# Experts put in order of their tokens, with two products a block where they have at most 64

## The chip, the cores and the metric

The kernel runs on one core of one Trainium2 chip, as one program. The metric is the device time of one execution in microseconds (us), the median of several runs. A profile of one further execution gives the span from its first to its last instruction, and every instruction of each engine: TensorE (PE, its weight loads PEld), VectorE (DVE), ScalarE (ACT), GpSimd (POOL) and SyncE (SP), which issues the loads.

## What is computed

Two stacks of two layers each over 256 tokens of width 1024, in float32. The change concerns the last layer's mixture of experts: eight experts, each a gated feed forward with 3584 inner columns; every token takes the two experts with the largest router logits.

```python
def moe_ffn(h, router_w, router_b, w_gate, w_up, w_down):
    t = h.reshape(b * s, d)
    logits = (t @ router_w).astype(jnp.float32) + router_b.astype(jnp.float32)
    top_vals, top_idx = lax.top_k(logits, TOP_K)
    top_w = jax.nn.softmax(top_vals, axis=-1)
    gates = jnp.sum(jax.nn.one_hot(top_idx, N_EXPERTS) * top_w[..., None], axis=1)
    out = jnp.zeros((b * s, d), jnp.float32)
    for e in range(N_EXPERTS):
        y = swiglu_2(t, w_gate[e], w_up[e], w_down[e])   # (silu(t @ g) * (t @ u)) @ d
        out = out + gates[:, e:e + 1] * y
    return out
```

The inputs are drawn at random from a seed, the default being 0. 256 tokens with two experts each are 512 choices, 64 an expert on average.

## The kernel before

**Float32 from two halves.** The large products take operands rounded to a shorter format (F32R in the code) in place of plain float32. Each operand is split into a high part (its rounding) and a low part (what is left), and one product becomes three: high with high, low with high, high with low. For the weights this is `halves` (lines 323 to 333): from each load of 128 x 1024 floats (0.524 MB) ScalarE writes `hi` (line 331) and VectorE `lo` (line 332). Both pools have three buffers (`hip`, `lop`), and a buffer comes free when TensorE has read it.

**Loads.** `load_half` (line 314, the DMA on line 320) issues a load on SyncE's queue into the next buffer of a ring; the ring for the experts has 27 buffers, and 6 more for the first expert's first blocks (`rawd`, `rawf`). The weights' order in memory is that of their use, and their addresses are fixed in the program. A load waits until VectorE has read the buffer's last content.

**The stage.** `route` (line 1552) makes the residual with tokens on partitions (`ACC`), its normed rows as high and low parts (`HH`, `HL`), the router's logits, the gates `GT`, and `key`: the slot that each token has at each of its experts, from 1 on, else 0. `experts` (line 1667) goes through the experts in the order of their numbers. `gather` turns `key` into a one-hot matrix `OH` (tokens by slots, line 1691) and multiplies `HH` and `HL` by it, so that `XG` holds an expert's tokens in up to 128 slots, features on partitions, both parts. It runs for the first expert alone, then for the second, and then for two at a time. Then come seven blocks of 512 inner columns. `gate_up` makes the gate's and the other product of a block: 2 x 8 x 3 products of a 128 x 128 stationary `XG` tile with 512 moving columns of weights. `down` transposes the gated result (4 transposes), splits it into `hh` and `hl` and adds 2 x 4 x 3 products into the expert's output `ya`; it is issued one block late, behind the next block's `gate_up`. That is 72 products and 12 loads a block, whatever number of the 128 slots is filled. After the seventh block `scatter` splits `ya` (two splits), brings it back to token order with `OT`, the transposed one-hot (8 products), and adds it to `ACC` with the gate (four VectorE operations, line 1781).

`moe` (line 1809) reads the largest count into a register and runs a second pass, for slots 129 to 256, only where an expert has over 128 tokens. `final` is the last norm. The order of instructions on each engine is fixed when the program is built, by a planner; at run time each engine works through its queue in order, and semaphores do the rest.

Of the kernel before, what the change touches and what calls it, by code (L numbers as in the profile page):

```python
# [18 lines left out]
P = 128  # L19
S = 256  # L20
# [7 lines left out]
# ---------------------------------------------------------------- column layout of the packed vectors  # L28
# [29 lines left out]
NRB, NRC, NRD, NRE, NRF = 8, 12, 4, 3, 2  # L58

# ---------------------------------------------------------------- constants of the shapes  # L60
# [3 lines left out]
def _const_arrays():  # L64
# [30 lines left out]
    add("iota", np.broadcast_to(i[None, :] + 1, (P, P)))  # L95
    add("rev8", np.broadcast_to(8.0 - np.arange(8)[None, :], (P, 8)))
    add("dmask", np.where(i[:, None] <= i[None, :], 0.0, -1.0e30))
# [25 lines left out]
    # trailing means less the token itself: tokens s of a first tile to t of both, and of a second to its own  # L123
# [16 lines left out]
# ---------------------------------------------------------------- host layout  # L140
# [22 lines left out]
def _pack(inp):  # L163
# [9 lines left out]
    for l in range(2):  # L173
# [12 lines left out]
        # an even head's turned rows come after its others, an odd one's before  # L186
# [21 lines left out]
    # key and query, value, and gate tiles, in the order of the heads' work  # L208
# [34 lines left out]
# ---------------------------------------------------------------- kernel  # L243
class _K:
# [12 lines left out]
    # ---- tensor engine  # L257
# [21 lines left out]
    # ---- constants  # L279
# [27 lines left out]
    # ---- weights  # L307
# [15 lines left out]
    def halves(self, raw, parts=1):  # L323
        """A weight's two parts."""
# [28 lines left out]
    # ---- splits and norms  # L353
# [47 lines left out]
    def prep(self, gname, gi):  # L401
        """Splits of x * g for all feature tiles, and the row scale to apply after the product."""
# [9 lines left out]
    # ---- dense feed forward  # L412
# [35 lines left out]
    # ---- rope tables  # L448
    def rope_tables(self, pool):
        nc = self.nc  # L450
        with self.tc.tile_pool(name="rope", bufs=1) as rp:
# [17 lines left out]
            for j in range(4):  # L469
                # phase of a quarter turn for the cosines  # L470
# [71 lines left out]
    def weave(self, *gens):  # L542
        """Issues the steps of several generators in turn: next the one whose steps weigh least so far."""
# [35 lines left out]
    def track(self, tag, gen, weight=1.0, ahead=0):  # L579
        """Runs a generator's steps with their PSUM banks under one tag."""  # L580
# [15 lines left out]
    def seg(self, fn, *args, **n):  # L596
        """Runs a stage with PSUM banks besides the products' two: for each tag its number."""
# [1340 lines left out]
```

## Time and profile before

| What | us |
|---|---|
| Median of 3 runs | 2648.29 |
| Lowest and highest run | 2646.78, 2648.96 |
| Span of the profiled execution | 2645.7 |
| TensorE busy in that span | 2605.0 |
| VectorE busy | 2001.3 |
| ScalarE busy | 1610.3 |

The profiled execution has no time of its own besides its span; the span lies 2.6 us below the median of the runs, which also hold what lies before the first and after the last instruction. An engine's busy time counts its instructions' own spans; a TensorE record holds the latency of its product too, so that records overlap. `L332` is line 332 of the kernel before; a line may be a helper's, so groups are told apart by the names of tiles: `gu` and `y` are the two kinds of products of a block, `x` the small products (transposes, gather, scatter).

### The profile page before, as it was taken

Reading aid. Unit: us, or ns where it says so; the run is one execution under the profiler, and the core shown is the slowest. Engines: PE = TensorE matmul, PEld = TensorE weight load, DVE = VectorE, ACT = ScalarE, POOL = GpSimd, SP = SyncE. Lnnn points to the kernel's source line nnn. Section 1 sums busy time; section 2 is a strip of 40 time slices with the busy share of each in tenths; the row PEclk is TensorE's granted clock in tenths of the full one; section 3 lists DMA queues with packets and bytes.
Section 4 is the critical chain, followed back from the end, with each engine's and each line's share of the span. In section 5 each row is a group of like instructions: output and inputs, shape, how many; then the busy total and the mean of one; then the engine's idle time right before and its main releaser. Section 6 shows DMA issues by size and latency. Waiting matters only on the chain.

```text
span 2645.7 us, 44986 instructions
## 1 busy us (share of the span) xinstructions
PE 2605.0 (98%) x17519; PEld 2365.1 (89%) x17519; DVE 2001.3 (76%) x2624; ACT 1610.3 (61%) x2208; POOL 86.7 (3%) x85
## 2 busy tenths in 40 slices
PE   8999999999999999999999999999999999999997
PEld 8999899999999899999999988888888888888886
DVE  7658567656658577656666867898989898989897
ACT  5444455444444555455445766777777777777776
POOL 0003000000003000000000200000000000000000
PEclk9999999999999999999999999999999999999999
DMA  6554125555554125555555339899999999999992
GB/s 232 190 183 160 56 79 163 187 184 184 185 184 159 62 81 172 187 185 167 188 187 166 120 132 338 312 336 355 336 367 354 341 351 364 352 340 354 363 353 96
DMA packets 166621, 602.08 MB, mean 228 GB/s; under 512 B 18704, under 2 KB 19232, under 8 KB 166400
## 3 DMA queue, kind: packets, MB, share of 16 engines
q1 hardware_dynamic: 165792, 596.92, 64.5%
q8 instruction: 139, 2.28, 0.3%
q0 software_dynamic: 608, 2.21, 0.3%
q14 instruction: 82, 0.67, 0.1%
HBM read 596.96 MB, written 1.05 MB: 226 GB/s over the span
## 4 chain that ended last, share of the span: by engine, by line
PE 93%; issue 3%; DVE 2%; ACT 1%; DMA 0%; POOL 0%; DVEq 0%; SPq 0%; ACTq 0%; POOLq 0%
PE m L259 24%; PE mm L259 23%; PE gu L259 22%; PE y L259 11%; PE s L259 6%; PE t L259 3%; PE x L259 1%; PE x L277 1%; PE s L500 1%; DVE lo L332 1%; PE u L259 1%; ACT hi L331 0%; PE c L259 0%; PE s L277 0%; ACT xh L360 0%
## 5 line engine op out<-in xcount | busy, mean ns | idle before, releaser
L331 ACT ACTIVATE hi<-raw 128x1024 fp32r<-128x1024 f32 x1128 | 1176.1, 1055 | 824.2 <-issue 323.3
L332 DVE TENSOR_TENSOR lo<-raw,hi 128x1024 fp32r<-128x1024 f32 x1128 | 1356.0, 1222 | 422.7 <-ACT hi L331 417.7
L259 PE MATMUL gu<-hi,XG 128*128 128x512 f32 x1792 | 559.9, 397 | 0.1
L259 PE MATMUL m<-xh,hi 128*128 128x256 f32 x1760 | 495.2, 281 | 9.2 <-ACT xh L360 8.7
L259 PE MATMUL m<-xh,lo 128*128 128x256 f32 x1760 | 495.4, 282 | 3.0 <-DVE lo L332 3.0
L259 PE MATMUL m<-xl,hi 128*128 128x256 f32 x1760 | 494.9, 281 | 1.8 <-DVE xl L361 1.8
L259 PEld LDWEIGHTS gu<-hi,XG 128*128 128x128 f32 x1792 | 337.1, 189 | 80.3 <-ACT hi L331 0.6
L259 PE MATMUL gu<-lo,XG 128*128 128x512 f32 x896 | 348.0, 398 | 0.0
L259 PEld LDWEIGHTS m<-xh,hi 128*128 128x128 f32 x1760 | 333.0, 189 | 9.8 <-ACT xh L360 9.1
L259 PEld LDWEIGHTS m<-xh,lo 128*128 128x128 f32 x1760 | 332.9, 189 | 3.9 <-DVE lo L332 3.9
L259 PEld LDWEIGHTS m<-xl,hi 128*128 128x128 f32 x1760 | 332.7, 189 | 2.4 <-DVE xl L361 2.4
L259 PE MATMUL mm<-hl,hi 128*128 128x256 f32 x880 | 248.2, 282 | 0.0
L259 PE MATMUL mm<-hh,lo 128*128 128x256 f32 x880 | 248.2, 282 | 0.0
L259 PE MATMUL mm<-hh,hi 128*128 128x256 f32 x880 | 247.6, 282 | 0.0
L259 PE MATMUL mm<-xh,hi 128*128 128x256 f32 x832 | 240.8, 290 | 6.1 <-DVE x L1128 3.2
L259 PE MATMUL mm<-xl,hi 128*128 128x256 f32 x832 | 239.9, 289 | 0.0
L259 PE MATMUL mm<-xh,lo 128*128 128x256 f32 x832 | 238.2, 287 | 0.1
L259 PEld LDWEIGHTS gu<-lo,XG 128*128 128x128 f32 x896 | 169.0, 189 | 41.4 <-DVE lo L332 0.9
L259 PE MATMUL y<-lo,hh 128*128 128x512 f32 x448 | 181.0, 404 | 0.0
L259 PE MATMUL y<-hi,hh 128*128 128x512 f32 x448 | 177.7, 397 | 0.7 <-ACT hh L357 0.7
L259 PE MATMUL y<-hi,hl 128*128 128x512 f32 x448 | 178.0, 397 | 0.0
L259 PEld LDWEIGHTS mm<-hl,hi 128*128 128x128 f32 x880 | 168.2, 191 | 0.0
(551 smaller groups left out, 3448.3 us busy)
## 6 DMA issues: line engine op xcount, KB each, us to landing
raw<-in_moe SPq DMA_DIRECT2D x668, 512.0 KB, 5.3
raw<-in_ffn SPq DMA_DIRECT2D x330, 512.0 KB, 4.2
raw<-in_win SPq DMA_DIRECT2D x56, 512.0 KB, 3.6
raw<-in_dnin SPq DMA_DIRECT2D x32, 512.0 KB, 3.5
raw<-in_wout SPq DMA_DIRECT2D x16, 512.0 KB, 3.5
raw<-in_pin SPq DMA_DIRECT2D x8, 512.0 KB, 4.3
raw<-in_dnout SPq DMA_DIRECT2D x8, 512.0 KB, 3.6
raw<-in_moe SPq DMA_DIRECT2D x8, 256.0 KB, 5.5
```

What stands on the lines that cost most here:

```text
L259: ins = self.nc.tensor.matmul(out, lhsT=lhsT, rhs=rhs, start=start, stop=stop)
L277: self.nc.tensor.transpose(out, in_, self.c("ident"))
L331: nc.scalar.activation(hi[:, c], raw[:, c], AF.Copy)
L332: nc.vector.tensor_tensor(lo[:, c], raw[:, c], hi[:, c].bitcast(F32), OP.subtract)
L500: nc.tensor.transpose(p4[:, h, :].bitcast(F32R), YP[:, h, 1, :], self.identr)
```

## The change

`route` also counts: which experts have over 64 tokens, and in which order the experts stand by their count, the first kept first (it gets 2 x 256 added). Place p gets the expert of rank `PLACES[p]`, so ranks 1 and 2 stand at places 3 and 6; the six other places are those of `FEW`. The keys and gates are brought into the order of the places (`keyp`, `GTp`); `keyl` is the key with 64 added. Three kinds of numbers go into registers: the largest count, whether the new form is valid (`ok`: at most two experts over 64, the first not among them, and none over 128), and the experts of places 1 to 7, with which SyncE addresses the loads.

`short` is a new form of `experts`. At a place of few tokens the high parts of the tokens stand in slots 1 to 64 of the stationary tile and the low parts in slots 65 to 128, so that one product by the weights' high part makes two of the three, and one by the low part the third (and the fourth, low with low, which was left out before). The gate's two halves of rows are added by a plain float32 product with `BOTH` (twice the identity of 64) before the gating; `down` adds them in its transposes, which become plain float32 products of 64 columns, and packs high and low parts into `hh`; `scatter` adds the halves of the output, its one-hot having both. A block at such a place has 48 products and the added ones in place of 72. At the two other places nothing changes. Where `ok` is 0, the residual, which has been copied to memory, is loaded again, and the whole of `experts` runs as before in a further pass. The early ring has 31 buffers in place of 33 (`NRD` 3 for 4, `NRF` 1 for 2). `experts` is kept for the further pass, with one gather for each expert. Two constants are added (a tile of zeros and the places). All other lines of the diff take comments away.

```diff
-NRB, NRC, NRD, NRE, NRF = 8, 12, 4, 3, 2
+NRB, NRC, NRD, NRE, NRF = 8, 12, 3, 3, 1
+PLACES = (0, 3, 4, 1, 5, 6, 2, 7)
+FEW = [r not in (1, 2) for r in PLACES]
...
-        cm = self.T(keep, [P, 1], "cm")
-        nc.vector.tensor_reduce(cm, pc[:, 0:8], AX.X, OP.max)
-        ci = self.T(keep, [P, 1], "ci", I32)
-        nc.vector.tensor_copy(ci, cm)
+        cnt = self.T(pool, [P, NE], "cnt")
+        nc.vector.tensor_copy(cnt, pc[:, 0:8])
+        many = self.T(pool, [P, NE], "many")
+        nc.vector.tensor_scalar(many, cnt, 64.5, None, OP.is_gt)
+        cv = self.T(pool, [P, 4], "cv")
+        nc.vector.tensor_reduce(cv[:, 0:1], cnt, AX.X, OP.max)
+        nc.vector.tensor_reduce(cv[:, 2:3], many, AX.X, OP.add)
+        nc.vector.scalar_tensor_tensor(cv[:, 2:3], many[:, 0:1], 8.0, cv[:, 2:3], OP.mult, OP.add)
+        nc.vector.tensor_scalar(cv[:, 3:4], cv[:, 0:1], P + 0.5, None, OP.is_lt)
+        nc.vector.scalar_tensor_tensor(cv[:, 1:2], cv[:, 2:3], 2.5, cv[:, 3:4], OP.is_lt, OP.mult)
...
+        nc.vector.tensor_scalar(cnt[:, 0:1], cnt[:, 0:1], 2.0 * S, None, OP.add)
...
+        nc.vector.tensor_tensor(same, other, own, OP.is_equal)
+        nc.vector.tensor_tensor(more, other, own, OP.is_gt)
+        nc.vector.tensor_tensor(same, same, low, OP.mult)
+        nc.vector.tensor_tensor(more, more, same, OP.add)
...
+        nc.vector.tensor_reduce(crank, more, AX.X, OP.add)
...
+        nc.vector.tensor_tensor(at, crank[:, None, :].broadcast_to([P, NE, NE]),
+                                self.c("places")[:, :, None].broadcast_to([P, NE, NE]), OP.is_equal)
+        nc.vector.tensor_tensor(more, at, rev[:, None, :].broadcast_to([P, NE, NE]), OP.mult)
+        nc.vector.tensor_reduce(cnt, more, AX.X, OP.add)
+        nc.vector.tensor_scalar(ci[:, 2:], cnt, -1.0, 8.0, OP.mult, OP.add)
...
+        keyp = placed(key, "keyp")
...
+        nc.vector.tensor_scalar(keyl, keyp, 0.5, 64.0, OP.is_gt, OP.mult)
+        nc.vector.tensor_tensor(keyl, keyl, keyp, OP.add)
+        GTp = placed(GT, "GTp")
...
+    def short(self, HH, HL, ACC, RS, keyp, keyl, GTp, BOTH, where, st):
...
+                    nc.vector.tensor_scalar(OH[:, t, u, :], self.c("iota"), keyp[:, t, e:e + 1], None, OP.is_equal)
+                    nc.vector.tensor_scalar(OL[:, t, u, :], self.c("iota") if FEW[e] else self.c("zero"),
+                                            keyl[:, t, e:e + 1] if FEW[e] else 1.0, None, OP.is_equal)
...
+                    for i, (src, one) in enumerate(((HH, OH), (HL, OL))):
+                        for t in range(2):
+                            self.mm(ps, o, src[:, t, c], one[:, t].rearrange("p a b -> p (a b)"), i + t == 0, i + t == 2)
...
+        def gate_up(e, fb, XG, RX):
...
+                    ch = self.chunk(where(e)[fb * 6 + m * 2 + q])
...
+                        self.mm(ps, ps, XG[:, 0, k, :], wh[:, c], k == 0, False)
+                        if not FEW[e]:
+                            self.mm(ps, ps, XG[:, 1, k, :], wh[:, c], False, False)
+                        self.mm(ps, ps, XG[:, 0, k, :], wl[:, c], False, k == DT - 1)
+                gu.append(ps)
+                if m == 0 and FEW[e]:
+                    both = self.T(pool, [P, 512], "both")
+                    nc.scalar.activation(both, ps, AF.Copy)
+            if FEW[e]:
+                self.mm(gu[0], gu[0], BOTH, both, True, True)
+            sl = self.T(pool, [P, 512], "sl")
+            nc.scalar.activation(sl, gu[0], AF.Silu, scale=RX)
+            nc.vector.scalar_tensor_tensor(sl, gu[1], RX, sl, OP.mult, OP.mult)
...
+        def down(e, fb, sl, ya, OT):
...
+                for i in range(4):
+                    self.mm(ps, p4[:, i, n], sl[:, i * P:i * P + P], BOTH[:, n], True, True)
+                self.split(p4[:, :, n], hh[:, :, n], hh[:, :, 64:])
...
+                    self.mm(ya[n], ya[n], hh[:, i, :], wh[:, c], first, False)
+                    if not FEW[e]:
+                        self.mm(ya[n], ya[n], hl[:, i, :], wh[:, c], False, False)
+                    self.mm(ya[n], ya[n], hh[:, i, :], wl[:, c], False, last)
...
+        ok = nc.values_load(ci[0:1, 1:2], min_val=0, max_val=1)
+        sp = mybir.EngineType.SP
+        order = [nc.values_load(ci[0:1, 2 + e:3 + e], engines=(sp,), min_val=0, max_val=NE - 1) for e in range(1, NE)]
+        moe = self.A["moe"]
+
+        def where(e):
+            return moe[bass.ds(order[e - 1], 1)][0] if e else moe[0]
...
+        back = [nc.dram_tensor(f"residual{t}", (P, D), F32).ap() for t in range(2)]
+        for t in range(2):
+            nc.gpsimd.dma_start(back[t], ACC[:, t, :])
+        with ExitStack() as st:
+            self.short(HH, HL, ACC, RS, *few, where, st)
+            self.final(ACC)
...
+        with tc.If(ok < 1):
+            for t in range(2):
+                nc.sync.dma_start(ACC[:, t, :], back[t])
+            run(0)
+            with tc.If(most > P):
+                run(P)
```

## Rows read from the trace of the kernel before

**Rows 1.** The page: busy time and its share of the span, by engine.

```profile
span 2645.7 us, 44986 instructions
...
PE 2605.0 (98%) x17519; PEld 2365.1 (89%) x17519; DVE 2001.3 (76%) x2624; ACT 1610.3 (61%) x2208; POOL 86.7 (3%) x85
```

**Rows 2.** Stretches: PE, PEld, DVE, ACT, POOL busy us, clock, DMA share, GB/s.

```profile
1660.00:2600.00 940.00, 940.00 (x4213) 760.31 (x4212) 843.72 (x819) 714.02 (x780) 0.00 (x0) 1.00 0.95 347
```

**Rows 3.** The chain in order of time, experts' stage: start us, us, what.

```profile
1674.08 9.84 PE gu L259 x42
...
1691.38 9.84 PE gu L259 x42
...
1758.74 4.22 PE y L259 x18
...
1886.84 4.22 PE y L259 x18
...
2009.81 4.22 PE y L259 x18
```

**Rows 4.** Waits from 1660 to 2600 us: total us, times, longest.

```profile
ACT hi L331 <- PE gu L259: 120.4, 220, 2.0
DVE lo L332 <- ACT hi L331: 91.3, 190, 1.4
```

**Rows 5.** Waits of SyncE's own queue, the same stretch.

```profile
SPq L320 <- DVE lo L332: 660.7, 605, 7.4
```

**Rows 6.** Timeline of TensorE around 1563 us: plain float32 products.

```profile
1563.36 1.06 PE L259 MATMUL s<-dS,kq 128*128 128x128 f32 x8
```

**Rows 7.** Groups by line and shape, 1660 to 2600 us: busy, mean ns.

```profile
L332 DVE TENSOR_TENSOR lo<-raw,hi 128x1024 fp32r<-128x1024 f32 x631 | 750.4, 1221 | 95.5 <-ACT hi L331 91.3 <-DMA raw<-in_moe 3.1 <-PE x L277 0.4
L331 ACT ACTIVATE hi<-raw 128x1024 fp32r<-128x1024 f32 x631 | 655.0, 1057 | 221.6 <-PE gu L259 120.4 <-PE y L259 85.3 <-DVE lo L332 9.7
...
L1741 DVE SCALAR_TENSOR_TENSOR sl<-gu,RX,sl 128x512 f32<-128x512 f32 x52 | 38.7, 744 | 0.0
...
L358 DVE TENSOR_TENSOR hl<-x,hh 128x512 fp32r<-128x512 f32 x52 | 35.5, 683 | 0.0
```

**Rows 8.** Timeline of VectorE, 1889 to 1911 us.

```profile
1888.88 2.42 DVE L332 TENSOR_TENSOR lo<-raw,hi 128x1024 fp32r<-128x1024 f32 x2
...
1893.80 1.22 DVE L332 TENSOR_TENSOR lo<-raw,hi 128x1024 fp32r<-128x1024 f32 x1 [0.76 <-ACT hi L331]
...
1903.85 0.68 DVE L358 TENSOR_TENSOR hl<-x,hh 128x512 fp32r<-128x512 f32 x1
1904.45 2.35 DVE L332 TENSOR_TENSOR lo<-raw,hi 128x1024 fp32r<-128x1024 f32 x2
1906.72 0.74 DVE L1741 SCALAR_TENSOR_TENSOR sl<-gu,RX,sl 128x512 f32<-128x512 f32 x1
1907.38 3.53 DVE L332 TENSOR_TENSOR lo<-raw,hi 128x1024 fp32r<-128x1024 f32 x3
```

**Rows 9.** Stretches of 5 us before the first block; columns as above.

```profile
1575.00:1580.00 5.00, 4.15 (x36) 3.89 (x35) 4.25 (x8) 1.28 (x8) 1.01 (x1) 1.00 0.01 3
1580.00:1585.00 5.00, 3.27 (x18) 2.92 (x17) 3.61 (x9) 2.60 (x12) 1.01 (x1) 0.78 0.00 0
...
1600.00:1605.00 5.00, 5.00 (x46) 5.00 (x45) 3.89 (x7) 4.67 (x10) 0.00 (x0) 1.00 1.03 415
...
1620.00:1625.00 5.00, 5.00 (x23) 4.71 (x23) 1.89 (x7) 0.60 (x1) 0.00 (x0) 0.54 1.03 417
```

**Rows 10.** Timeline of VectorE as the first one-hot is made.

```profile
1617.13 0.28 DVE L1625 TENSOR_TENSOR tie<-tie,low 128x128 f32<-128x128 f32 x1
1617.45 0.29 DVE L1626 TENSOR_TENSOR cmp<-cmp,tie 128x128 f32<-128x128 f32 x1
...
1618.74 0.16 DVE L1648 TENSOR_REDUCE m<-l 128x2 f32<-128x16 f32 x1
```

**Rows 11.** Operations on raw tiles from 1500 us: ns min/median/max.

```profile
L320 SPq DMA_DIRECT2D raw<-in_moe x676: 327/328/1410, 1560.4 to 2588.5; - x169
```

More of the change, by code (lines that the diff above doesn't have):

```diff
@@ L95, in _const_arrays @@
     add("iota", np.broadcast_to(i[None, :] + 1, (P, P)))
+    add("zero", np.zeros((P, P)))
     add("rev8", np.broadcast_to(8.0 - np.arange(8)[None, :], (P, 8)))
+    add("places", np.broadcast_to(np.array(PLACES, float)[None, :], (P, 8)))
     add("dmask", np.where(i[:, None] <= i[None, :], 0.0, -1.0e30))
@@ new lines, in route @@
+        nc.vector.tensor_reduce(cv[:, 0:1], cnt, AX.X, OP.max)
[3 more added lines that the diff above has]
+        nc.vector.scalar_tensor_tensor(cv[:, 1:2], cv[:, 2:3], 2.5, cv[:, 3:4], OP.is_lt, OP.mult)
+        ci = self.T(keep, [P, 2 + NE], "ci", I32)
+        nc.vector.tensor_copy(ci[:, 0:2], cv[:, 0:2])
@@ new lines, in route @@
+        nc.vector.tensor_scalar(cnt[:, 0:1], cnt[:, 0:1], 2.0 * S, None, OP.add)
+        other, own = [a.broadcast_to([P, NE, NE]) for a in (cnt[:, None, :], cnt[:, :, None])]
+        more, same = [self.T(pool, [P, NE, NE], n) for n in ("more", "same")]
+        nc.vector.tensor_tensor(same, other, own, OP.is_equal)
+        nc.vector.tensor_tensor(more, other, own, OP.is_gt)
+        nc.vector.tensor_tensor(same, same, low, OP.mult)
+        nc.vector.tensor_tensor(more, more, same, OP.add)
@@ new lines, in placed @@
+        def placed(src, name):
+            prod = self.T(pool, [P, 2, NE, NE], "placed")
+            nc.vector.tensor_tensor(prod, at[:, None].broadcast_to([P, 2, NE, NE]),
+                                    src[:, :, None, :].broadcast_to([P, 2, NE, NE]), OP.mult)
+            dst = self.T(keep, [P, 2, NE, 1], name)
+            nc.vector.tensor_reduce(dst, prod, AX.X, OP.add)
+            return dst.rearrange("p t a b -> p t (a b)")
+        keyp = placed(key, "keyp")
+        keyl = self.T(keep, [P, 2, NE], "keyl")
@@ L1667, in experts @@
+        nc.vector.tensor_scalar(keyl, keyp, 0.5, 64.0, OP.is_gt, OP.mult)
+        nc.vector.tensor_tensor(keyl, keyl, keyp, OP.add)
+        GTp = placed(GT, "GTp")
+        BOTH = self.T(keep, [P, 2, 64], "BOTH")
+        for i in range(2):
+            nc.vector.tensor_tensor(BOTH[:, i, :], self.c("ident")[:, 0:64], self.c("ident")[:, 64:128], OP.add)
+        return HH, HL, ACC, RS, GT, key, ci, (keyp, keyl, GTp, BOTH.rearrange("p a b -> p (a b)"))
     def experts(self, base, HH, HL, ACC, RS, GT, key, st):
@@ L1671, in open_ @@
             return st.enter_context(tc.tile_pool(name=f"{name}{base}", bufs=bufs))
-        pool, p1, px = open_("moe", 2), open_("moe1", 1), [open_("moex", 1)]
-        late = []
-        rooms = [0, 1, 2, 0, 1, 2, 0, 1]
-        if not base:
-            early = st.enter_context(ExitStack())
-            ringf = early.enter_context(tc.tile_pool(name="rawf", bufs=NRF))
-            self.once += [ringf] * NRF
+        pool, p1, px, py = open_("moe", 2), open_("moe1", 1), open_("moex", 1), open_("moey", 1)
         if base:
@@ L1772, in scatter @@
         def scatter(e, n, y, OT, end):
-            yh = self.T(late[0], [P, 512], f"yh{n}", F32R)
-            yl = self.T(late[0], [P, 512], f"yl{n}", F32R)
+            yh = self.T(py, [P, 512], f"yh{n}", F32R)
+            yl = self.T(py, [P, 512], f"yl{n}", F32R)
             self.split(y, yh, yl)
@@ L1785, in experts @@
         steps = [(e, fb) for e in range(NE) for fb in range(7)]
-        G = gather([0])
+        ya, pend = None, None
+        for e, fb in steps + [(None, None)]:
+            if e is not None:
+                if fb == 0:
+                    g, = gather([e])
+                sl = gate_up(e, fb, g[0], g[2])
+            if pend is not None:
+                pe, pf, psl, pg = pend
+                if pf == 0:
+                    ya = [self.T(self.psy, [P, 512], f"y{n}") for n in range(2)]
+                down(pe, pf, psl, ya, pg)
+            pend = (e, fb, sl, g[1]) if e is not None else None
@@ L1791, in experts @@
                     self.early.close()
-                    if not base:
-                        early.close()
-                    px += [open_("moex2", 1), open_("moex3", 1)]
-                    late.append(open_("moey", 1))
+                    early.close()
+                    px.append(open_("fewx2", 1))
+                    late.append(open_("fewy", 1))
                 sl = gate_up(e, fb, G[e][0], G[e][2])
@@ L1800, in experts, with moe @@
                     ya = [self.T(self.psy, [P, 512], f"y{n}") for n in range(2)]
-                down(pe, pf, psl, ya, pg[1])
-                if pf == 4 and pe == 0:
-                    G += gather([1])
-                elif pf == 4 and pe % 2 and pe < NE - 1:
-                    G += gather([pe + 1, pe + 2])
-            cur = G[e] if e is not None else None
-            pend = (e, fb, sl, cur) if e is not None else None
-    def moe(self, HH, HL, ACC, RS, GT, key, ci):
+                down(pe, pf, psl, ya, pg)
+                es = [1] if pe == 0 else [pe + 1, pe + 2] if pe % 2 and pe < NE - 1 else None
+                if pf == 4 and es:
+                    for _ in gather(es):
+                        pass
+            pend = (e, fb, sl, G[e][1]) if e is not None else None
+    def moe(self, HH, HL, ACC, RS, GT, key, ci, few):
         nc, tc = self.nc, self.tc
         most = nc.values_load(ci[0:1, 0:1], min_val=0, max_val=S)
+        ok = nc.values_load(ci[0:1, 1:2], min_val=0, max_val=1)
[5 more added lines that the diff above has]
+        back = [nc.dram_tensor(f"residual{t}", (P, D), F32).ap() for t in range(2)]
+        for t in range(2):
+            nc.gpsimd.dma_start(back[t], ACC[:, t, :])
+        with ExitStack() as st:
+            self.short(HH, HL, ACC, RS, *few, where, st)
+            self.final(ACC)
         def run(base):
@@ L1816, in run @@
                 self.final(ACC)
-        run(0)
-        with tc.If(most > P):
-            run(P)
+        with tc.If(ok < 1):
+            for t in range(2):
+                nc.sync.dma_start(ACC[:, t, :], back[t])
+            run(0)
+            with tc.If(most > P):
+                run(P)
     def squares(self, ACC, t, n):
```

105 lines of the change are left out of this document (103 added, 2 removed).

## The prediction, made before the changed kernel was run

> **What bounds the kernel now.** I read the page first: a span of 2645.7 us with TensorE busy 98% of it [rows 1]. That average says little here, because the change touches one stage alone, the mixture of experts, from about 1619 us on; so every other view is read for that stage. There the view by stretches shows TensorE busy without a gap at full clock, VectorE busy 844 of 940 us and ScalarE 714, while the DMA engines are busy 95% of the time at 347 GB/s [rows 2]. Four units are thus close together, and the question is which of them is the first to stop a shorter TensorE stage.
>
> The chain of work in order of time names the limit: it is TensorE's products, block after block. A block (512 of an expert's 3584 columns) starts its 42-product run every 17.30 us, and 42 products take 9.84 us, 0.234 us each [rows 3]. 72 products a block make 16.87 us, the four transposes the rest. Scatter and gather come on top: two experts last 251.07 us, 125.5 each, where 7 blocks alone are 121.1 [rows 3]. The waits agree: ScalarE's high part waits for a product to give back its buffer (120.4 us), and VectorE's low part for ScalarE (91.3 us) [rows 4]. Both are held back by TensorE and not the other way round. SyncE likewise waits 660.7 us for VectorE to free a raw buffer [rows 5]: the loads have room to run faster than they are asked to.
>
> **The change, part by part.** *Products.* At the six places of few tokens (42 of 56 blocks) 72 products become 48: 11.25 us at 0.234 us. Added is one plain float32 product with 512 moving columns. The nearest row is float32 of 128 columns, 8 records in 1.06 us [rows 6], so some 0.112 us a record (the last one's 0.28 us of latency taken off), and the code issues half as many such products as there are records; four times the columns give 0.90 us. The four transposes become float32 products of 64 columns, at most 0.90 us by the same row. With each expert's scatter (8 products, 1.87 us) and half of a pair's gather (the first of the two experts lasts 128.10 us and the second 122.97, so 5.1 a pair [rows 3]) TensorE needs about 13.7 us a block, where a block now takes 17.93 with its share of both. TensorE stops being the limit; what is late next must be found.
>
> *VectorE.* Its work on the weights stays: twelve low parts a block. One lasts 1221 ns [rows 7], but back to back two take 2.35 us [rows 8], so one is worth 1.14 and twelve 13.7. The gated product is worth 0.66 (1906.72 to 1907.38) and the split 0.60 (1903.85 to 1904.45) [rows 8], of which half the columns remain: 0.30 by the columns, and I take 0.33 for what is fixed. That is 14.7 us. Per expert come two splits and four additions of the scatter (3.8 us) and about 1.9 us of one-hots, copies and the sum of both one-hots: 0.8 a block. VectorE's floor is 15.5 us a block, 108.4 an expert.
>
> *ScalarE.* Twelve high parts at 1057 ns [rows 7] are 12.7 us even when nothing overlaps, and a copy, a gate and half a split, none longer than VectorE's 744 ns for 512 columns [rows 7], add at most 1.9; the scatter's two splits and some three copies of the gather, taken at the same 744 ns, add 0.5 a block. 15.1 is thus an upper bound, under VectorE.
>
> *Loads.* Twelve loads of 0.524 MB are 6.29 MB a block, now 364 GB/s in a plain block. When many buffers were free, before the first block, the five windows from 1600 to 1625 us show 403 to 417 GB/s [rows 9]. At 410 a block's loads take 15.3 us, an expert's 107.4. So VectorE and the DMA engines have the same floor within 1%.
>
> *How near the floor it gets.* From 1888.88 to 1910.91 VectorE worked off a backlog with 0.76 us idle in 22.0 [rows 8], with the same three buffers of each part: 96.5% is reachable. 108.4 / 0.965 is 112.3; since the loads are equally tight and neither covers for the other, I add 2 us and take 114.5 an expert. Six experts at 125.5 - 114.5 = 11.0 save 66 us. The bounds are 108.4 (no idle; 103 us saved) and 125.5 (nothing saved).
>
> *Places of many tokens.* Two experts keep their 72 products and stay bound by TensorE: 0 us, their loads covered by full buffers.
>
> *Sorting.* Some 22 small VectorE operations stand between the counts and the first one-hot. Dependent operations on 128 elements start 0.32 us apart (1617.13, 1617.45), and a short one lasts 0.16 [rows 10]; with 14 of them dependent, most on 64 elements, at about 0.25 and the rest at some 0.1 (they overlap), the first one-hot moves by 4 us (bounds 2 and 9: all overlapped, and all 22 dependent with a few waits between them). TensorE waits there already, so it is on the path: +4.
>
> *Register addresses.* SyncE reads nine values and computes each load's address. No row has such a load; the nearest are its fixed ones, median 328 and longest 1410 ns [rows 11]. At the median, a block's twelve issues take 3.9 us under 15.3 of transfer: nothing. At the longest they take 16.9, and that would be the new limit. I take the lower, as nearly all rows lie there. A wait of SyncE for the sorted order holds up the loads queued behind it; 31 buffers are filled or ordered by then, two and a half blocks, which cover it: 0. Two buffers fewer in the early ring (33 to 31) would cost 2.6 us of transfer if VectorE emptied it; the DMA pace around 1620 us makes that unlikely: 0. The residual's copy to memory is 1.05 MB, 2.6 us of DMA time, hidden by the same buffers; GpSimd's queue issues nothing else in this stage. The further pass isn't run unless the counts ask for it (below), and the end of the kernel is unchanged.
>
> Sum: 2645.7 - 66 + 4 = 2583.7 us of span. The median of the runs lies 2.6 above the span (2648.3), so 2586.
>
> **The DMA rule.** The rows above show loads at 403 to 417 GB/s for 25 us [rows 9]. The Trainium skill, "DMA: Bandwidth & Descriptors", section "Where 436 GB/s comes from", says that between HBM and SBUF a core is held to about 358 GB/s. By that figure a block's loads would take 17.6 us, a few-token expert 123.0, and the sum would come to about 2637 us. The trace disagrees: 347 GB/s is a mean with waits in it, and the burst is 15% above the rule.
>
> **The rivals.** *The loads keep today's pace.* A burst of 25 us need not last 1000 us: the stage's mean with 95% DMA share is 347 GB/s [rows 2]. If 364 GB/s is what long running gives, an expert takes 121.1 us: 6 x 4.4 = 26 saved, 4 lost, 2626 us. The same band holds the case of the slow register issue (118.4 an expert: 2610). For it speaks the high share; against it that SyncE's queue waits for buffers and not for transfers [rows 5]. The rule weighed above (the Trainium skill, "DMA: Bandwidth & Descriptors", "Where 436 GB/s comes from") falls into this band too.
>
> *The buffer loop eats the gain.* A high part's buffer lives from ScalarE (1.06) over VectorE (1.22) to the last product that reads it (about 0.7): 3.0 us for three buffers, so there is 0.4 us of slack in three low parts at 1.14. The float32 product (0.9) and the four small ones (0.9) stand in TensorE's queue ahead of the products that give buffers back. If neither they nor ScalarE's extra copy are absorbed, a block takes 15.5 + 2.3 = 17.8 and the result is 2647: no change. Against it speaks the stretch at 96.5%, which holds scatter products and ScalarE's splits.
>
> *The other side: a further pass.* The two-product form is valid while at most two experts exceed 64 tokens and the first doesn't. Counting the reference router's two choices over the 256 tokens of its default inputs gives 64, 59, 68, 59, 84, 64, 57, 57: valid, but two experts sit exactly at 64, and the two closest choices (logits 0.0005 and 0.0007 apart) would each put one of those at 65. One flipped token decides, and then the whole stage runs again: eight experts at 125.5 and a start, about +1010 us, 3600 or more. A lesser slow case is the clock: TensorE with gaps fell to 0.78 of full clock in one window with 3.27 us busy in 5 and stayed at 1.00 with 4.15 in 5 [rows 9]. 13.7 us in 16 is the better of these; at 1.2 GHz for more than 0.31 of the products of those blocks (13.7 x 1.31 = 17.9) the gain would be gone.
>
> **How the numbers follow.** What a measurement here can tell from no change is about 0.2%, 5.3 us. Forecast band 2550 to 2608 us: 0.56. Loads or their issue at the present pace, 2608 to 2642: 0.24. No change, within 5.3 us of 2648: 0.07. Slower: 0.13, of it 0.05 the further pass, 0.04 the clock, 0.04 an order of work or a wait that I don't see. The first two bands are the range, 2550 to 2642, and faster has 0.80. Its lower end is near the 108.4 floor (103 saved, 4 lost: 2549). The predicted time is that of the first case, 2586.
>
> **What would show it.** In the profile after, few-token experts last 112 to 117 us and the two others 123 to 128. In stretches of the former the loads move 380 to 395 GB/s, VectorE is busy above 95%, and TensorE shows gaps at an unchanged clock; VectorE's low parts no longer wait on ScalarE because of TensorE, and some wait for a load. TensorE has some 750 records fewer (42 x 24 products gone, 42 x 6 records added). The first one-hot comes 2 to 9 us after the key. The prediction is wrong if the span has two passes; if a few-token block is still at 17 us, with DMA share at 1.0 (the loads) or with ScalarE waiting for TensorE (the buffer loop); or if SyncE's issues stand a block's time apart without a wait (the addresses).

## The result, and the profile after

The changed kernel takes 2569.38 us (median of 4 runs, 2567.44 to 2571.28), the kernel before 2647.9 in the same job. The ratio is 0.970, 95% interval 0.969 to 0.972: faster by 78.5 us. The forecast was 2586 in a range from 2550 to 2642. The profiled execution has a span of 2568.6 us, 77.1 less than before. One kernel among the experiments, *fewer low parts, fourth buffers*, was profiled in a slow execution of 3450 us, at a granted clock of 0.65 (its four others took 2575 to 2578 us), so its places are not listed.

The page of the changed kernel, against [rows 1]:

```profile
span 2568.6 us, 44854 instructions
...
PE 2499.9 (97%) x16795; PEld 2195.2 (85%) x16795; DVE 1981.9 (77%) x2663; ACT 1615.1 (63%) x2260; POOL 88.4 (3%) x87
```

TensorE has 724 records fewer; VectorE and ScalarE do as much as before. Where the time went is read by place. The stretches below run from the first split of one place's output (`yh`) to that of the next: places 1 to 6, and the last. Places 3 and 6 hold the experts of many tokens. Columns as in [rows 2].

```profile
1748.57:1862.44 113.87, 110.06 (x474) 77.09 (x474) 111.03 (x123) 99.11 (x125) 0.00 (x0) 1.00 1.00 388
1862.44:1972.95 110.51, 107.65 (x430) 73.47 (x431) 107.58 (x105) 95.49 (x107) 0.00 (x0) 1.00 1.02 401
1972.95:2099.33 126.38, 125.74 (x567) 100.26 (x567) 114.01 (x119) 95.32 (x107) 0.00 (x0) 1.00 0.97 350
2099.33:2209.60 110.27, 106.24 (x417) 69.11 (x417) 107.16 (x104) 94.21 (x107) 0.00 (x0) 1.00 1.01 398
2209.60:2325.60 116.00, 111.79 (x488) 79.51 (x488) 109.72 (x115) 97.51 (x123) 0.00 (x0) 1.00 1.00 385
2325.60:2448.16 122.56, 121.46 (x524) 95.23 (x525) 111.12 (x106) 95.14 (x101) 0.00 (x0) 1.00 0.98 359
2448.16:2550.70 102.54, 97.53 (x383) 64.49 (x384) 98.76 (x100) 85.71 (x102) 0.00 (x0) 0.98 0.71 277
```

In the few-token places VectorE is busy 95 to 98% of the time (107.58 of 110.51), and the granted clock is 1.00. TensorE, which had no gap in [rows 2], has gaps now. Its column still reads as high as VectorE's (107.65 of 110.51), but its records hold latency: one block's products are worth 12.9 us (worked out below) of the 15.3 that a block takes. The columns alone thus don't say which of the two sets the pace; the waits and the experiments do. In the kernel before, the same seven stretches lasted 128.09, 122.96, 128.04, 122.96, 128.04, 122.96 and 112.48 us (a gather for two experts runs in places 1, 3 and 5).

The waits from 1640 to 2540 us (who, for whom: total us, times, longest), against [rows 4]:

```profile
PEld gu L265 <- DVE lo L338: 98.1, 223, 1.1
ACT hi L337 <- PE y L265: 57.1, 94, 2.3
ACT hi L337 <- PE gu L265: 48.3, 95, 2.0
DVE lo L338 <- ACT hi L337: 39.4, 84, 1.5
...
DVE lo L338 <- DMA raw<-in_moe: 0.3, 1, 0.3
```

The longest is new: TensorE's weight load waits for VectorE's low part (0.7 us in the kernel before). VectorE waits for ScalarE 39.4 us, where it was 91.3, and for a load once, for 0.3 us.

### The profile page after: what moved, and what is told of

It is laid out like the page before. It is cut to its first block, busy times and chain, and to the rows that moved or that the text cites. A ratio compares the mean times of both kernels' runs of the same rounds, so it can differ in the third digit from the quotient of the medians.

```text
span 2568.6 us, 44854 instructions
## 1 busy us (share of the span) xinstructions
PE 2499.9 (97%) x16795; PEld 2195.2 (85%) x16795; DVE 1981.9 (77%) x2663; ACT 1615.1 (63%) x2260; POOL 88.4 (3%) x87
## 5 line engine op out<-in xcount | busy, mean ns | idle before, releaser
L265 PE MATMUL gu<-lo,XG 128*128 128x512 f32 x896 | 393.4, 441 | 14.4 <-DVE lo L338 10.9
L265 PE MATMUL gu<-hi,XG 128*128 128x512 f32 x1120 | 403.6, 397 | 0.4 <-ACT hi L337 0.4
L265 PEld LDWEIGHTS gu<-hi,XG 128*128 128x128 f32 x1120 | 211.8, 189 | 48.5 <-issue 10.1
L265 PEld LDWEIGHTS mm<-hh,lo 128*128 128x128 f32 x880 | 168.4, 191 | 0.0
```

What stands on the lines that cost most here:

```text
L265: ins = self.nc.tensor.matmul(out, lhsT=lhsT, rhs=rhs, start=start, stop=stop)
```

## The experiments

Twelve further kernels ran. "Few-token places" below are 1 and 2 (the first with a pair's gather), 4 and 5 (the second with one); their lengths come from each profile as above. Nearly every edit made the planner write the instructions of this stage in another order. The traces show the same order on ScalarE, VectorE and TensorE for three pairs: the changed kernel and *fewer loads* up to place 3, *fewer low parts* and *fewer of both* into place 2, and the changed kernel and the short pass of *the further pass*. Every other comparison holds the edit and a new order together.

| Kernel | Median us | Ratio to before, interval | Places 1, 2, 4, 5 (us) |
|---|---|---|---|
| the changed kernel | 2569.4 | 0.970 [0.969, 0.972] | 113.9, 110.5, 110.3, 116.0 |
| fewer low parts | 2582.0 | 0.975 [0.974, 0.977] | 109.3, 113.7, 118.0, 119.4 |
| fewer loads | 2565.1 | 0.969 [0.967, 0.970] | 113.9, 110.5, 108.3, 114.4 |
| fewer of both | 2542.5 | 0.960 [0.959, 0.962] | 109.3, 106.5, 104.9, 110.7 |
| all places with three products | 2671.1 | 1.009 [1.008, 1.011] | 133.4, 123.0, 123.0, 132.8 |
| fourth buffers | 2566.2 | 0.969 [0.968, 0.971] | 114.3, 110.6, 109.9, 114.9 |
| fewer low parts, fourth buffers | 2577.0 | 0.973 [0.972, 0.975] | - |
| fewer of both, fourth buffers | 2508.0 | 0.948 [0.946, 0.950] | 105.2, 99.5, 99.2, 107.4 |
| no adding of the gate's halves | 2563.4 | 0.969 [0.967, 0.970] | 111.3, 108.9, 109.3, 115.0 |
| fewer low parts, two `hh` | 2575.1 | 0.972 [0.970, 0.973] | 109.6, 110.6, 114.1, 117.7 |
| one low part in twelve on GpSimd | 2600.9 | 0.982 [0.980, 0.983] | 121.5, 116.1, 115.4, 118.8 |
| the further pass | 3605.2 (one run) | - | 113.9, 110.5, 110.3, 116.0 |
| four buffers and casts | 2563.9 | 0.968 [0.966, 0.969] | 113.5, 111.3, 109.9, 115.7 |

### Who sets the pace: VectorE, the loads, or both

Three kernels take work from VectorE, from the loads, and from both, at the few-token places. With *fewer low parts* 3 of a block's 12 low parts are not made and the high part stands for them; with *fewer loads* 3 of its 12 loads are not made and the neighbour's data stand for them.

```diff
+    def halves_hi(self, raw):
+        hi = self.T(self.hip, [P, 1024], "hi", F32R)
+        self.nc.scalar.activation(hi, raw, AF.Copy)
+        return hi, hi
...
     def chunk(self, ap, less=False):
         raws, self.head = self.head or [self.load_half(ap, j) for j in range(2)], None
-        return [self.halves(r) for r in raws]
+        return [self.halves(raws[0]), self.halves_hi(raws[1]) if less else self.halves(raws[1])]
...
```

*Fewer low parts.*

> In the few-token blocks three of the twelve weight tiles get no low part from VectorE (TensorE reads the high part in its place, so one of the four terms is wrong for a quarter of the weights); loads, ScalarE and TensorE work as before. VectorE loses 3 x 1.14 = 3.4 us a block, its floor falls from 108.4 to about 84 us an expert. Theory 1, VectorE sets the pace and the loads are close behind it: a few-token expert falls from 112.7 to the loads' floor of about 108 us, six times 4 to 5 us, 2539 to 2546 us. Rival 2, the loads set the pace: no change, 2565 to 2573. Rival 3, the loop over three buffers and TensorE's added products set it: part of the loop is gone too (three tiles a block skip VectorE's 1.22 us), 2555 to 2565.

*Fewer loads.*

```diff
-        raws, self.head = self.head or [self.load_half(ap, j) for j in range(2)], None
-        return [self.halves(r) for r in raws]
+        raws, self.head = self.head or [self.load_half(ap, j) for j in range(1 if less else 2)], None
+        return [self.halves(r) for r in (raws * 2 if less else raws)]
...
```

> In the few-token blocks three of the twelve loads are left out (the tile before is split a second time, so a quarter of these weights are wrong); all work of VectorE, ScalarE and TensorE stays. The DMA engines need 80.5 us an expert in place of 107.4. Theory 1, VectorE sets the pace: 2560 to 2571 us, a few-token expert stays at 110 to 113. Rival 2, the loads set it: an expert falls to VectorE's floor of 108.4, 2540 to 2550. Rival 3, the buffer loop: no change, 2565 to 2573.

*Fewer of both* (both edits).

> Both together: three of twelve loads and three of twelve low parts are left out in the few-token blocks (a quarter of these weights are wrong). Theory 1 and rival 2 alike: the pace falls to the next limit, TensorE at 13.7 or ScalarE at 13 to 15 us a block, 96 to 105 us an expert, 2470 to 2525 us. Rival 3, the buffer loop with the added products in it: the loop is shortened in a quarter of the tiles only, 2545 to 2565.

Measured: without a quarter of the loads the time falls by 4 us, and places 1 and 2, where the order of instructions is that of the changed kernel, keep their lengths to 0.01 us. So the loads don't set the pace; the 2.0 and 1.6 us by which places 4 and 5 get shorter come with another order. Without a quarter of the low parts the kernel gets *slower* by 12.6 us, which none of the expectations has, although place 1 falls from 113.9 to 109.3 us. Without both it gains 27 us: much less than Theory 1 has, and nearest to Rival 3, the loop over the buffers (2545 to 2565 us).

First, the loads. SyncE's issues in the changed kernel, 1640 to 2517 us (ns min/median/max; then DMA from issue to landing):

```profile
L326 SPq DMA_DIRECT2D raw<-in_moe x636: 327/333/617, 1642.4 to 2516.6; - x159
L326 SPq MOVE raw<-in_moe x592: 29/29/38, 1697.3 to 2515.9; - x198
...
DMA to landing us min/median/max: 3.2/6.1/8.0
```

How far they are ahead is a count. Loads issued up to 2200 us, and high parts that ScalarE made of them up to then (groups by line, 1618 to 2200 us):

```profile
L326 SPq DMA_DIRECT2D raw<-in_moe x446: 327/333/1251, 1560.9 to 2199.3; - x149
```

```profile
L337 ACT ACTIVATE hi<-raw 128x1024 fp32r<-128x1024 f32 x418 | 429.9, 1055 | 74.6 <-PE y L265 35.7 <-PE gu L265 32.7 <-DMA raw<-in_moe 0.4
```

Three high parts of the experts' weights had been made before 1618 us (at 1601.91, 1607.83 and 1610.60), so 421 are used, and 446 - 421 = 25 loads are ahead of ScalarE, of a ring of 27; at 1900 us it is 229 - 204, the same. One chunk is used every 1.27 us (15.26 us a block, the distance of two `both` copies, over 12), so a load is issued some 32 us before its use and lands in 6. SyncE waits for VectorE to free a buffer (483.3 us in this stage; it was 660.7 in [rows 5]): the loads go at VectorE's pace, though the DMA share reads 1.00.

That the loads cost nothing is shown directly by place 1 of two kernels, *fewer low parts* and *fewer of both*. Both programs issue the instructions of ScalarE, VectorE and TensorE there in the same order (it is the same from the start of the kernel into place 2), and only the loads differ:

```profile
1746.30:1855.57 109.27, 106.75 (x476) 77.45 (x475) 88.57 (x101) 98.00 (x125) 0.00 (x0) 1.00 1.02 407
```

```profile
1749.43:1858.71 109.28, 106.88 (x476) 77.55 (x475) 88.57 (x101) 98.02 (x126) 0.00 (x0) 1.00 0.89 303
```

407 against 303 GB/s, and 109.27 against 109.28 us. From within place 2 on (1903 us) the planner wrote the two programs in different orders. In place 4, one block of ScalarE with *fewer low parts*:

```profile
2131.75 0.38 ACT L368 ACTIVATE hh<-x 128x256 fp32r<-128x256 f32 x1 [0.98 <-PE y L265]
2132.03 2.00 ACT L337 ACTIVATE hi<-raw 128x1024 fp32r<-128x1024 f32 x2
2133.92 1.05 ACT L343 ACTIVATE hi<-raw 128x1024 fp32r<-128x1024 f32 x1
2135.16 1.06 ACT L337 ACTIVATE hi<-raw 128x1024 fp32r<-128x1024 f32 x1 [0.19 <-PE gu L265]
2137.47 0.60 ACT L1931 ACTIVATE both<-gu 128x512 f32<-128x512 f32 x1 [1.25 <-PE gu L265]
...
2146.57 1.06 ACT L337 ACTIVATE hi<-raw 128x1024 fp32r<-128x1024 f32 x1 [1.00 <-PE y L265]
2148.61 0.38 ACT L368 ACTIVATE hh<-x 128x256 fp32r<-128x256 f32 x1 [0.98 <-PE y L265]
```

and with *fewer of both*:

```profile
2134.64 1.06 ACT L343 ACTIVATE hi<-raw 128x1024 fp32r<-128x1024 f32 x1 [0.19 <-PE y L265]
2136.70 3.16 ACT L337 ACTIVATE hi<-raw 128x1024 fp32r<-128x1024 f32 x3 [1.00 <-PE y L265]
2139.76 0.37 ACT L368 ACTIVATE hh<-x 128x256 fp32r<-128x256 f32 x1
2140.03 1.05 ACT L343 ACTIVATE hi<-raw 128x1024 fp32r<-128x1024 f32 x1
2140.98 2.20 ACT L337 ACTIVATE hi<-raw 128x1024 fp32r<-128x1024 f32 x2
2143.29 0.60 ACT L1931 ACTIVATE both<-gu 128x512 f32<-128x512 f32 x1
```

The first has four high parts between `hh` and `both`, the second three. In the first, ScalarE waits for TensorE in each block at `hh`, at the fourth high part, at `both` and at a high part of the down products (1.00), and a block takes 16.86 us (2131.75 to 2148.61); in the second the waits of 1.00 and 0.19 are left, and two `both` copies stand 14.75 us apart. So *fewer low parts* loses in the places where its written order differs, and not by its loads: from 1640 to 2540 us its VectorE waits for a load once.

```profile
DVE lo L338 <- DMA raw<-in_moe: 1.6, 1, 1.6
```

The next two runs ask whether a shortage of buffers makes that order slow.

*Fewer low parts, fourth buffers* (the edit of the fourth buffers is below).

> The run in which 3 of 12 low parts of a few-token block are not made (their high part stands in for them), with the fourth buffers added. That run was 12 us slower than the changed kernel with less work. Theory A (there the high-part buffer is held until the second of its two products is done, so the loop of three buffers stops ScalarE): with four buffers the loss is gone, 2550 to 2568, few-token experts under 112. Theory B (the loads in that run: a DMA share of 1.00 at 372 GB/s in the later experts): four buffers change nothing, 2576 to 2588, few-token experts still 114 to 119 on the later places.

*Fewer low parts, two `hh`.*

```diff
-            hh = self.T(p1, [P, 4, P], "hh", F32R)
+            hh = self.T(pool, [P, 4, P], "hh", F32R)
```

> The run in which 3 of 12 low parts of a few-token block are not made, which took 2582 and in its later experts came to a steady 16.9 us a block, with 17 loads issued ahead of ScalarE all along. One thing more is changed: the split hidden vector (the tile hh) gets two buffers for one (the ring of loaded chunks is one shorter). Theory A (in that run each block stops ScalarE about 1 us at the write of hh, until the last products of the block before have read it, and the stop goes round through the high parts, the low parts and TensorE): without it the later experts stay at the pace of the first, 105 to 110, and the time is 2535 to 2560. Theory B (the loads, which stood at a DMA share of 1.00 there): no change, 2576 to 2588.

The text above says 17 loads ahead; that count took along high parts of the dense layer before, and counted as above it is some 25. Measured: 2577.0 and 2575.1, 5 and 7 us better, of some 40 that lie between *fewer low parts* and *fewer of both*. Neither Theory A holds. Theory B has the times (the second to 1 us) but named the loads, and the pair of place 1 and the single wait for a load speak against that. What stays is the order. That it is the cause is inferred and not shown: a run of *fewer low parts* in the other's order was not tried, so which of its differences counts is open.

### The loop of three buffers

```diff
-        hi = self.T(self.hip, [P, 1024], "hi", F32R)
-        lo = self.T(self.lop, [P, 1024], "lo", F32R)
+        self.nh += 1
+        four = self.hi4 is not None and self.nh % 4 == 3
+        hi = self.T(self.hi4 if four else self.hip, [P, 1024], "hi", F32R)
+        lo = self.T(self.lo4 if four else self.lop, [P, 1024], "lo", F32R)
```

> The changed kernel with a fourth buffer for the high parts and a fourth for the low parts in the experts' stage (the ring of loaded chunks is two buffers shorter for it). Theory 1 (VectorE and the loads set the pace together, 97% and a DMA share of 1.00): the fourth buffer has nothing to give, 2569 within 6 us, few-token experts 111 to 114 us. Rival (the loop of three buffers, in which ScalarE waits 105 us for TensorE's products, sets the pace): those waits fall under 40 us and the few-token experts fall to about 109, 2545 to 2560.

> The run with 3 of 12 low parts not made and 3 of 12 loads left out (2542.5), with the fourth buffers added. If the loop of three buffers is what stopped that run at 104 to 110 us per few-token expert, the waits of VectorE for ScalarE's high part (134 us) fall by more than half, experts come to 96 to 101, and the time to 2485 to 2520. If TensorE's own products (97% busy as modelled) set it, nothing moves: 2538 to 2546.

In the changed kernel the fourth buffers bring 3 us, within Theory 1's 6 and not clear of noise: ScalarE's waits for TensorE's products fall from 105.4 to 68.7 us (49.1 and 19.6; the rival has under 40), and the places keep their lengths within 1.1 us. VectorE is full. With fewer of both they bring 34.5 us, and place 2 falls from 106.5 to 99.5 us:

```profile
1842.39:1941.87 99.48, 97.97 (x430) 75.81 (x429) 87.19 (x86) 91.78 (x108) 0.00 (x0) 1.00 0.96 343
```

So with less work for VectorE the next pace is 106.5 us an expert, some 4 us below its 110.5, and the loop of three buffers is the likeliest reason. With fourth buffers TensorE's weight loads hardly wait for low parts any more (103.8 us without them, 10.5 with them). But the order of instructions changed too, and one sign is missing: VectorE's waits for ScalarE's high part, which were to fall by more than half, fell from 133.7 to 99.9 us. What holds the last version is not told apart here: ScalarE works 91.8 of the 99.5 us, and TensorE about as much (seven blocks of 12.9, worked out below, are 90.5).

### The gate's halves

Left out: the adding of the products with the tokens' low part to the gate.

```diff
-                if m == 0 and FEW[e]:
-                    both = self.T(pool, [P, 512], "both")
-                    nc.scalar.activation(both, ps, AF.Copy)
-            if FEW[e]:
-                self.mm(gu[0], gu[0], BOTH, both, True, True)
```

> The changed kernel without adding the two halves of the gate's products: two BOTH products and ScalarE's copy of 587 ns are left out of each few-token block (of 41), so gate and up are incomplete. Theory 1: off the bounding engines (VectorE 97%, loads 1.00), so 2569 down to 2560. Rival (TensorE idles in the round trip from its products over ScalarE and back, which the prediction's buffer loop has in it): some 1.2 us a block, 2515 to 2530.

2563.4, 6 us less: Theory 1. In the rival it would be 1.2 us in each few-token block (there are 42). The prediction's buffer loop had the product and the copy in it; they are absorbed, but for 0.14 us a block.

### What the new order and addresses cost by themselves

All places keep three products; sorting, places, register addresses and the further pass's test stay (and the ring is one shorter).

```diff
-FEW = [r not in (1, 2) for r in PLACES]
+FEW = [False for r in PLACES]
```

> Sorting, places and register addresses stay, but all eight places take three products a block (the ring has one buffer less, 26 for 27). If the gain is the fewer products alone: 2648 to 2654 us, that is the time before and the 2 to 4 us of sorting. If the order of the experts or the new gather gives a part of the gain: 2620 to 2640. If the register addresses cost something that the gain has hidden: above 2660.

Measured: 23 us slower than before. That is the band which the expectation gave to the register addresses, but the places show another reason. By place, from the first to the second split as above:

```profile
1769.55:1902.91 133.36, 132.01 (x617) 107.62 (x616) 115.02 (x123) 99.59 (x127) 0.00 (x0) 1.00 0.92 331
1902.91:2025.88 122.97, 122.97 (x541) 99.03 (x540) 110.91 (x105) 93.73 (x102) 0.00 (x0) 1.00 0.97 359
```

Place 2, all loads by register address, takes 122.97 us, to 0.01 what it took in [rows 3]: there the addresses cost nothing. Place 1 takes 5.3 us more than its 128.10 there, and the two others with a pair's gather 5.3 and 4.7: for places of many tokens the new gather makes the low part's product by itself, 32 more products of 128 columns (`x<-OH,HL`, 5.2 us busy in place 1). With 7.7 us up to place 1 (sorting, the first gather in that form, the shorter ring) this is the 23 us. The fewer products, with the gather that goes with them, are thus worth 2671.1 - 2569.4 = 102 us, and the kernel pays for the rest out of it.

### The further pass

```diff
-nc.vector.tensor_scalar(many, cnt, 64.5, None, OP.is_gt)
+nc.vector.tensor_scalar(many, cnt, 63.5, None, OP.is_gt)
```

> The changed kernel with the bound on a place's tokens at 63.5 in place of 64.5, so that three experts count as many, where two places are wide, and the further full pass over all experts runs behind the short one. By the prediction's rival of the further pass, some 1010 us more than 2569 (the experts' stage of the kernel before, with its loads not ahead of it): 3560 to 3640. If the short pass could be broken off, about 2650.

```profile
span 3603.4 us, 58524 instructions
...
PE 3526.6 (98%) x21419; PEld 3025.5 (84%) x21419; DVE 2890.2 (80%) x3544; ACT 2388.7 (66%) x3098; POOL 89.1 (2%) x88
```

3605.2 us in a single run, 1036 more than the changed kernel. The short pass runs to its end (places as long as ever) and the whole stage after it. The rival's price was 1010. By the counts in the prediction it is four experts, not three, that have over 63.5 tokens, the first among them; either is enough for the further pass.

### Two tries to go further

*One low part in twelve on GpSimd*, which does nothing in this stage.

```diff
+        if gp:
+            nc.scalar.activation(hi, raw, AF.Copy)
+            nc.gpsimd.tensor_tensor(lo, raw, hi.bitcast(F32), OP.subtract)
+            return hi, lo
```

> The changed kernel, complete, with one of the 12 low parts of a few-token block made by GpSimd in a low-part buffer of its own, a fourth high-part buffer, two hh buffers, and a ring of loaded chunks three shorter. If VectorE's 15.5 us a block alone sets the pace, and loads do not (they stand 17 ahead, and land in 6 us), VectorE's work falls by 1.22 a block to 14.3 and ScalarE with 15 is the next limit: 0.5 to 0.9 us a block over 41 blocks, 2533 to 2552. If the loads set the pace with VectorE, 2563 to 2570. If a low part on GpSimd (2.78 us for its own 128x1024 product elsewhere in the kernel) holds up TensorE, slower than 2570.

It is 31 us slower than the changed kernel. GpSimd's and VectorE's timelines, 1765 to 1792 us:

```profile
1769.91 2.42 POOL L337 TENSOR_TENSOR lo<-raw,hi 128x1024 fp32r<-128x1024 f32 x1 [17.16 <-ACT hi L336]
1785.51 2.38 POOL L337 TENSOR_TENSOR lo<-raw,hi 128x1024 fp32r<-128x1024 f32 x1 [13.19 <-ACT hi L336]
```

```profile
1766.37 3.49 DVE L343 TENSOR_TENSOR lo<-raw,hi 128x1024 fp32r<-128x1024 f32 x3
...
1770.77 4.91 DVE L343 TENSOR_TENSOR lo<-raw,hi 128x1024 fp32r<-128x1024 f32 x3
...
1785.67 5.57 DVE L343 TENSOR_TENSOR lo<-raw,hi 128x1024 fp32r<-128x1024 f32 x3
```

Three low parts take VectorE 3.49 us, and 4.91 and 5.57 while GpSimd makes one: 1.4 and 2.1 us lost for the 1.22 saved. GpSimd's two ended 1.56 and 2.22 us after VectorE's began (1772.33 and 1787.89 us), which is about what VectorE lost. The Trainium skill, "SBUF — State Buffer", section "SBUF: two separate sides", says that GpSimd and a VectorE operation with two inputs in SBUF share one pair of ports, which one of them holds for its whole instruction while the other stands. These rows agree. TensorE waits for GpSimd's low part besides, as the third reading of the expectation has it (1640 to 2540 us):

```profile
PEld y L265 <- POOL lo L337: 25.2, 22, 3.3
```

How the 31 us divide between the two is not told apart. The added buffers are not the cause: the next kernel has them too and is the faster one.

*Four buffers and casts*: the fourth buffers, two `hh`, and the casts of a pair's gather on ScalarE.

```diff
-                    if (k // nk + u) % 2:
+                    if w == 2 or (k // nk + u) % 2:
```

> The changed kernel, complete, with what helped it or should: a fourth high-part and a fourth low-part buffer, two hh buffers, and in the gathers of two experts every cast of the sorted rows on ScalarE (VectorE's 21 casts take 6.9 us in the experts' stage); the ring of loaded chunks is four shorter, so some 13 ahead. Theory 1 (VectorE alone sets the pace of the few-token places; loads that land in 6 us need no 17 ahead): the 3 us of the fourth buffers and up to 5 of the casts, 2558 to 2566. Rival (fewer chunks ahead cost, or ScalarE with the added casts comes to its limit in the gathers): 2568 or more.

2563.9 (2559.5 to 2565.6, 5 runs) against 2569.4: as Theory 1, and the fastest kernel here that leaves nothing out, by 0.2%, with intervals that overlap. With 20 loads ahead (226 issued, 206 used at 1900 us, four of these before 1618) nothing is lost.

## Why the prediction was right, point by point

**TensorE stops being the limit, VectorE is next.** Right. One block of TensorE in place 4:

```profile
2156.81 1.02 PE L265 MATMUL gu<-both,BOTH 128*128 128x512 f32 x2
2157.27 0.80 PE L265 MATMUL gu<-lo,XG 128*128 128x512 f32 x1
2157.91 0.39 PE L265 MATMUL gu<-hi,XG 128*128 128x512 f32 x1
...
2161.99 1.00 PE L265 MATMUL x<-BOTH,sl 128*128 128x64 f32 x8
2162.80 0.48 PE L265 MATMUL y<-hi,hh 128*128 128x512 f32 x1
```

From the product with `BOTH` to the product after the next are 1.10 us, one of the usual 0.23 among them: 0.87, where 0.90 was taken. The four small ones take 0.81 of the 0.90. With 11.25 for the 48 products a block is 12.9.

**VectorE's floor of 108.4 us an expert.** Right: its busy time in places 1, 2, 4 and 5 is 111.0, 107.6, 107.2 and 109.7, 108.9 on average.

**112.3 and 2 us more.** The four places last 112.7 us on average, which is 108.4 / 0.965 without the addition. The step that failed is "since the loads are equally tight and neither covers for the other". They run at VectorE's pace, 25 buffers ahead. The span came out 2583.7 - 2568.6 = 15.1 us under the sum, and this step is the largest part of it: places 1, 2, 4 and 5 saved 51.4 us where 44 were forecast, 7.4 more. The first place saved 15.5 (127.1 from its first gather product, before 142.6) where 11 were forecast, the last 9.9. The rest is 1.75 from sorting, 2.1 from the places of many tokens and 0.5 behind the last place.

**Sorting, +4.** It was 2.25 on the path, by TensorE's first gather product, which was at 1619.24 before:

```profile
1621.49 1.08 PE L265 MATMUL x<-OH,HH 128*128 128x128 f32 x4 [3.89 <-DVE OH L1866]
```

The key and the first one-hot on VectorE, before and after:

```profile
1618.58 0.17 DVE L1638 SCALAR_TENSOR_TENSOR key<-s,sel 128x16 f32<-128x16 f32 x1
1618.82 0.47 DVE L1691 TENSOR_SCALAR OH<-c_dn,key 128x128 fp32r<-128x128 f32 x2
```

```profile
1617.58 0.17 DVE L1644 SCALAR_TENSOR_TENSOR key<-s,sel 128x16 f32<-128x16 f32 x1
1621.06 0.47 DVE L1866 TENSOR_SCALAR OH<-c_dn,keyp 128x128 fp32r<-128x128 f32 x2
```

The one-hot comes 3.48 us after the key, where it was 0.24: sorting costs 3.24, close to the 4. That the key was ready 1.00 us sooner made it 2.25; nothing in the prediction has that, and its cause is open.

**Many-token places, 0.** They got 1.7 and 0.4 us shorter (126.38 and 122.56). **Register addresses, 0.** Right, by place 2 of the kernel with three products everywhere. The issue's median went from 328 to 333 ns, with a register move of 29 ns beside it; twelve of both are 4.3 us of a block's 15.3. **The ring, the residual's copy, 0.** Not measured by themselves; neither VectorE nor ScalarE waits for a load from 1615 to 1760 us.

**The rivals.** *The loads keep today's pace*: they moved 385 to 401 GB/s in the few-token places, and 407 for 109 us in one experiment. The Trainium skill's "DMA: Bandwidth & Descriptors", section "Where 436 GB/s comes from", holds a core to about 358 GB/s between HBM and SBUF. These rows, with one core at work, disagree. *The buffer loop*: not the limit here, as the fourth buffers show; likely the next one. *The further pass*: not run, and as dear as said (1036 for 1010). *The clock*: 1.00 in the six stretches before the last place, 0.98 in it.

**What would show it.** VectorE's share (94.6 to 97.5%), the clock and the one-hot came as said, and TensorE has 724 records fewer for some 750. Places 2 and 4 (110.5 and 110.3 us) came out under the 112 to 117 and their load rates (401 and 398 GB/s) over the 380 to 395: the same step again, which had the places too long. Place 6 (122.6) is just under the 123 to 128. Two signs did not come. VectorE's low parts still wait for ScalarE (39.4 us), and none waits for a load beyond once 0.3 us, which was the sign that would have gone with the 2 us.

## What to carry to other kernels

A DMA share of 1.00 doesn't make the loads a limit: count the loads issued and the chunks used, and look at what the issuing queue waits for, before adding a second limit to the first. When an engine's work is taken away in an experiment and the time rises, compare a stretch where the instruction order is the same in both programs, since a planner may have written another one. Behind the limit that is removed the next ones stand close (here VectorE at 110.5 us an expert and, with less work for VectorE, 106.5), so a gain is sized by the second limit and not by the work removed.

## What had not been expected

Low parts on GpSimd cost VectorE at least as much as they save it: 36 of the 41 took 3.15 us each on average (the shortest 2.37), and VectorE's own, some 630, went from 1.22 to 1.32 on average; they are 41 fewer. And a load rate of 407 GB/s with 1.02 of DMA share, beside 303 with 0.89, made a difference of 0.01 us in a place of the same order.
